# A hybrid decoder trunk: some products of its layers come out transposed, with the weight matrix standing in the array

## The chip, the cores and the metric

One core of a Trainium2 chip runs the whole program. The metric is the device time of one execution in microseconds (us). A change of about 0.3% is the least that runs of this kernel can tell from none.

## The reference, cut to what matters

Two layers (l = 0, 1) over 256 positions of width 1024, in float32. Per layer:

```python
mod = silu(c) @ ada_w[l] + ada_b[l]                 # shift1, scale1, gate1, shift2, scale2, gate2
h = rms_norm(x, norm_mix_w) * (1 + sc1) + sh1
proj = h @ w_in                                     # u,v | fox q,k,v | moba q,k,v | z, xbc | gates
y_a = gmlp(gelu(u), gelu(v))                        # uses u, v by position
y_b = forgetting_attention(q, k, v, f)              # scores q @ k.T: needs q and k with channels on partitions
y_c = moba_attention(rotary(q), rotary(k), v)       # 256 positions are one block: causal attention
y_d = mamba2(z, xbc, dt)                            # convolution along positions: needs channels on partitions
merged = sum(sigmoid(gate_i) * (y_i @ w_branch_i))
x = x + g1 * (merged @ w_out)
h = rms_norm(x, norm_mlp_w) * (1 + sc2) + sh2
x = x + g2 * (relu(h @ mlp_w1) ** 2 @ mlp_w2)       # D_FF = 4096: eight blocks of 512 columns
```

The output is `rms_norm(x)`.

## The kernel before

**Products.** Every large product runs in three float32r matmuls per term: an operand is split into a rounded part `hi` and a rest `lo`, and hi·hi, hi·lo and lo·hi are added in PSUM. The activations are held transposed (128 channels on the partitions, positions along the row) in pairs `xh`, `xl`. The weights stream: a load (`raw`, 512 KB) brings 256 rows by 512 columns of a weight matrix; ScalarE rounds it into `hi` (L363), VectorE subtracts to get `lo` (L365), and TensorE uses the pair. Such a load with its matmuls is called a unit here. `unit_mms` (L415 to L421) does a unit for one half of the positions (t = 0 or 1, 128 positions each): 128 columns of `xh` or `xl` stand in the array as weights, and the 512 columns of `hi` or `lo` move through. A unit has 2 t x 2 j x 3 = 12 matmuls of 512 moving columns, each with its own load of 128 standing columns, and its result has positions on the partitions. `gemm` (L423) chains units into a product (4 units where 1024 rows are summed); `by_tile` takes all units of several products for t = 0 and then for t = 1, so that t = 0 is ready early.

**Where the result is wanted transposed.** Four kinds of results are turned behind the product by `transposes` (L505), four 128 x 128 TensorE transposes into one PSUM bank, twice per product of 512 columns:
- z and the Mamba inputs (`z0` to `z3`, four products per layer): `zx_post` (L667) copies PSUM to SBUF (L671), transposes (`zxT`), and copies out in pieces (L679, L681).
- q and k of the forgetting attention (`fq`, `fk`) and of the other one (`mq`, `mk`): `qk_post` (L593), with transposes named `fqt`, `fkt`, `mqt`, `mkt`.
- each block of the MLP's hidden layer (`w10` to `w17`): `hidden_post` (L900) takes relu and square (L904, L905) to `rl`, transposes to `hd`, and splits into `hh` and `hl` (L502, L503), which stand in the array in the second product (`yps`).

**MLP.** The blocks 0 and 1 of the first product run by tile, while the second half of h is still being normed. From b = 2 on, a turn of the loop does the second product of block b - 2 (four units into `yps`), and then the first product of block b (four units, `w1b`). The blocks 6 and 7 of the second product run by tile at the end.

**Order.** The queue of the loads (SyncE) is in the order of the code; on the other engines a scheduler sets the order at build time. Loads go into a ring of 5 `raw` buffers; `hi` and `lo` have 4 buffers each, and `ahead` (L380) asks for three units in advance. 20 units per layer near its joints borrow other tiles for `hi` and `lo` (`lent`, L287). Beside the weights of the products, 80 loads hold pieces of `ada_w`: VectorE alone uses them, in `ada_step` (L240, L242). They are spread over the stages (24 of them in the MLP of layer 0, 8 in that of layer 1).

Running generators (`start`, `pump`) emit the work behind a product step by step between its successors' units.

Of the kernel before, what the change touches and what calls it, by code (L numbers as in the profile page):

```python
# [7 lines left out]
F32 = mybir.dt.float32  # L8
# [10 lines left out]
NT = 2  # L19
# [119 lines left out]
def trunk_kernel(ctx: ExitStack, tc: tile.TileContext, a: dict, out: bass.AP):  # L139
# [283 lines left out]
    def gemm(key, nk, xs, ps=None, start=True, stop=True, alloc=gps):  # L423
        n = nk // 2
        if ps is None:
            ps = [alloc(f"ps_{key[0]}{key[1]}_{t}") for t in range(NT)]
        for u in range(n):
            i = take(key, 1)[0]
            ahead(i)
            for t in range(NT):  # L430
                unit_mms(i, t, ps[t], xs[t][0], xs[t][1], 2 * u, start and u == 0, stop and u == n - 1)
            pump()
        return ps

    def by_tile(parts):


        got = [take(p[0], p[1]) for p in parts]
        for t in range(NT):
            for (key, n, xs, bank, start_, stop_, after), ids in zip(parts, got):  # L440
                ps = bank(t)
                for u, i in enumerate(ids):
                    ahead(i, got[-1][-1] + 1 if t == 0 else None)
                    unit_mms(i, t, ps, xs[t][0], xs[t][1], 2 * u, start_ and u == 0, stop_ and u == n - 1)
                    pump()
                if after is not None:
                    after(t, ps)
# [43 lines left out]
    def xT_tiles(nm):
        r = []
        for t in range(NT):
            r.append((ap_.tile([P, KT, P], F32R, tag=f"xh{t}", name=f"xh{nm}{t}"),
                      ap_.tile([P, KT, P], F32R, tag=f"xl{t}", name=f"xl{nm}{t}")))
        return r

    def yT_tiles(nm, n, tag):
        return [[mp.tile([P, n, P], F32R, tag=tag, bufs=4, name=f"y{w}{nm}{t}") for w in "hl"] for t in range(NT)]

    def hilo(hi, lo, src):
        s.copy(hi, src)  # L502
# [90 lines left out]
    def qk_post(l, nm, part, ps, tT, rot):  # L593
        tks = []
        for t in range(NT):
            tk = tok(f"{nm}{part}{l}{t}")
            s.activation(tk, ps[t], AF.Copy, scale=0.125 if part == "q" else 1.0)
            if rot:
                k4 = tk.rearrange("p (h c) -> p h c", h=NH)[:, :, 0:16].rearrange("p h (a f) -> p h a f", a=2)
                ra = w2([P, NH, 2, 8], f"ra{part}{l}{t}")  # L600
                rb = w2([P, NH, 2, 8], f"rb{part}{l}{t}")
                cs = rope[:, t, 0, None, :].to_broadcast([P, NH, 16]).rearrange("p h (a f) -> p h a f", a=2)
                sn = rope[:, t, 1, None, :].to_broadcast([P, NH, 16]).rearrange("p h (a f) -> p h a f", a=2)
                v.tensor_tensor(ra, k4, cs, op=ALU.mult)
                v.tensor_tensor(rb, k4[:, :, ::-1, :], sn, op=ALU.mult)
                v.tensor_tensor(k4, ra, rb, op=ALU.add)
            tks.append(tk)
        yield 1
        for t in range(NT):
            tp = transposes(tks[t], f"{nm}{part}t{l}{t}")  # L610
            if t == 0:
                v.tensor_copy(tT[:, :, t * P:(t + 1) * P], tp)
            else:
                s.copy(tT[:, :, t * P:(t + 1) * P], tp)
            yield 0

    def qkv(l, nm, hT, rot):
        tr = []
        for part in ("q", "k"):
            ps = gemm((l, nm + part), KT, hT)  # L620
            tT = mp.tile([P, 4, 2 * P], F32, tag="qk", bufs=2, name=f"{nm}{part}T{l}")
            start(qk_post(l, nm, part, ps, tT, rot), -1)
            tr.append(tT)
        ps = gemm((l, nm + "v"), KT, hT)
        vt = []
        for t in range(NT):
            vt.append(tok(f"{nm}v{l}{t}"))
            s.copy(vt[t], ps[t])
        return tr[0], tr[1], vt
# [37 lines left out]
    def zx_post(l, n, ps, zs, xb):  # L667
        tks = []
        for t in range(NT):
            tk = tok(f"zx{l}{n}{t}")  # L670
            s.copy(tk, ps[t])  # L671
            tks.append(tk)
        yield 1
        for t in range(NT):
            tp = transposes(tks[t], f"zxT{l}{n}{t}")
            for lo_, hi_ in ((0, 2), (2, 4)):
                f0 = 4 * n + lo_
                if f0 < 6:
                    s.copy(zs[:, f0:f0 + 2, t * P:(t + 1) * P], tp[:, lo_:hi_, :])  # L679
                else:  # L680
                    s.copy(xb[:, f0 - 6:f0 - 4, 3 + t * P:3 + (t + 1) * P], tp[:, lo_:hi_, :])  # L681
            yield 0
# [217 lines left out]
    def hidden_post(l, b, pw, hb):  # L900
# [6 lines left out]
        for t in pw:  # L907
            tp = transposes(qs[t], f"hd{l}{b}{t}")
            hilo(hb[t][0], hb[t][1], tp)
            yield 0  # L910

    load_par(0, s)
    fullp = mp.tile([P, KT, 2 * P], F32, tag="s10", bufs=1, name="full0")
    hT = xT_tiles("h0")
    ccol = cst[:, K_C:K_C + KT]
    nr = [norm_sum(0, "a0")]
    cth = sp.tile([P, KT], F32, tag="cth", bufs=1, name="cth")
# [55 lines left out]
    for l in range(L):  # L975
# [64 lines left out]
            zx = [start(zx_post(l, 0, pz, zs, xb), -1)]  # L1040
        start(narrow(l, full, res))
        for n in range(1 if l == 0 else 0, 4):
            ps = gemm((l, f"z{n}"), KT, hT)
            zx.append(start(zx_post(l, n, ps, zs, xb), -1))
        g.memset(xb[:, :, 0:3], 0.0)
        gen_d = mamba(l, zs, xb, yd, res, zx)
        start(gen_d, 4)
# [50 lines left out]
        yc = yT_tiles(f"c{l}", 4, "y3")  # L1098
        gen_c.append(start(attention(f"m{l}", yc, qTm, kTm, vtm, None), 2))
        branch("b", yb, before=lambda: drain(gen_b[0]))  # L1100
        mT = xT_tiles(f"m{l}")

        def merge_T(t, q):
            tp = transposes(mg[t][:, q * 512:q * 512 + 512], f"mT{l}{t}{q}")
# [4 lines left out]
        def merge_gen(t, q):  # L1109
# [3 lines left out]

        branch("c", yc, before=lambda: drain(gen_c[0]),
               last=lambda t, n: start(merge_gen(t, n), 0 if t == 0 else 1))
        h2 = xT_tiles(f"h2{l}")

        def after_o(n):
            def f(t, ps):
# [7 lines left out]


        yps = [[gps(f"yps{l}{t}{n}") for n in range(2)] for t in range(NT)]
        hid = {}  # L1130

        def hidden_tiles(b):
            hid[b] = [[mp.tile([P, 4, P], F32R, tag="y2" if b % 2 else "y3", bufs=4, name=f"h{w}{l}{b}{t}")
                       for w in "hl"] for t in range(NT)]

        gens = []

# [9 lines left out]
        for b in range(2, 9):  # L1147
            for n in range(2) if b < 8 else ():
                p = b - 2
                gemm((l, f"w2{p}{n}"), 4, hid[p], ps=[yps[0][n], yps[1][n]], start=p == 0, stop=False)  # L1150
            if b < 8:
                pw = gemm((l, f"w1{b}"), KT, h2, alloc=xps)
                hidden_tiles(b)
                gen_h = start(hidden_post(l, b, dict(enumerate(pw)), hid[b]), -1)
            if b == 2 and l + 1 < L:
                load_big(l + 1, nc.sync)
            if b == 4 and l + 1 < L:
                start(spatial_sum(l + 1))
        if l + 1 < L:
            nh = xT_tiles(f"h{l + 1}")  # L1160
            nf = mp.tile([P, KT, 2 * P], F32, tag="s10", bufs=1, name=f"full{l + 1}")
            next_h = (nh, nf)

# [102 lines left out]
```

## Time and profile before

| | us |
|---|---|
| median of 3 runs | 1137.05 |
| lowest, highest | 1134.5, 1137.47 |
| the profiled execution's own time | 1135.02 |
| its span in the trace | 1133.3 |
| TensorE matmuls busy, in the span | 1099.9 |
| VectorE busy | 767.7 |
| ScalarE busy | 625.3 |

A matmul is shown from its start to the end of its way through the array, and it overlaps its successor; so what a matmul costs is read from start to start and not from its shown length. A weight load (PEld) begins when the matmul before it begins to stream, and this makes the starts of the loads the sharper clock where matmuls of unlike shapes follow each other.

The stages in the trace, by the names of TensorE's outputs: `u`, `v`, `z` to 101 us, `fq`, `fk`, `fv` to 137, the four branches to 355, `w_out` to 381, the MLP of layer 0 to 582, then the same for layer 1 (MLP from 937 to 1125).

### The profile page before, as it was taken

The numbers are of one execution on the slowest core, as the hardware profiler recorded it, in microseconds if no ns is written. First come the engines' busy times: TensorE is split into PE (matmuls) and PEld (weight loads), VectorE is DVE, ScalarE is ACT, GpSimd is POOL, SyncE is SP. The second block draws the span as 40 slices with busy tenths as digits, with TensorE's granted clock in tenths as the row PEclk, the third lists the DMA queues.
The fourth block names the chain that finished last, engine by engine and source line by source line (L and its number), as shares of the span: only waits on it lengthen the run. The fifth ranks groups of instructions, "written<-read, shape, count | busy, mean of one in ns | idle before, by whom it ended". The sixth has DMA issues, their size and how long they took to land.

```text
span 1133.3 us, 14903 instructions
## 1 busy us (share of the span) xinstructions
PE 1099.9 (97%) x5500; PEld 875.2 (77%) x5500; DVE 767.7 (68%) x1092; ACT 625.3 (55%) x1007; POOL 36.5 (3%) x58
## 2 busy tenths in 40 slices
PE   6999999999999999999899999999999999999997
PEld 4778877877777788887577888787777777888885
DVE  3785857886777856556677567679768586555555
ACT  4556765555654645544464676656555456544453
POOL 0000002000000100000000000110000001000000
PEclk9999999999999999999999999999999999999998
DMA  9865444576666567677745554446666654666661
GB/s 354 339 239 173 167 170 142 193 238 207 213 214 238 191 234 259 227 241 251 268 150 196 183 194 153 165 149 219 217 211 207 225 187 166 206 210 208 200 234 38
DMA packets 65321, 234.52 MB, mean 207 GB/s; under 512 B 7256, under 2 KB 8024, under 8 KB 65248
## 3 DMA queue, kind: packets, MB, share of 16 engines
q1 hardware_dynamic: 64960, 233.30, 60.2%
q8 instruction: 43, 0.70, 0.2%
q10 hardware_dynamic: 288, 0.27, 0.1%
q14 instruction: 30, 0.25, 0.1%
HBM read 232.49 MB, written 1.05 MB: 206 GB/s over the span
## 4 chain that ended last, share of the span: by engine, by line
PE 78%; DMA 10%; DVE 7%; ACT 2%; issue 2%; POOL 1%; DVEq 0%; POOLq 0%; ACTq 0%; SPq 0%
DMA raw<-in_wpk_dram 9%; PE yps L420 4%; PE yps L419 4%; PE yps L421 4%; DVE lo L365 3%; PE ps_1w L420 2%; PE ps_1w L419 2%; PE ps_1w L421 2%; PE ps_1z L419 1%; PE ps_0z L419 1%; PE ps_0w L419 1%; PE ps_0w L420 1%; PE ps_0z L421 1%; PE ps_1z L421 1%; PE ps_0w L421 1%
## 5 line engine op out<-in xcount | busy, mean ns | idle before, releaser
L363 ACT CAST hi<-raw 128x1024 fp32r<-128x1024 f32 x319 | 333.2, 1050 | 321.1 <-PE yps L421 66.4
L365 DVE TENSOR_TENSOR lo<-raw,hi 128x1024 fp32r<-128x1024 f32 x315 | 382.1, 1223 | 168.6 <-ACT hi L363 167.1
L242 DVE SCALAR_TENSOR_TENSOR acc<-raw,csil,acc 128x1024 f32<-128x1024 f32 x70 | 89.8, 1283 | 99.9 <-DMA raw<-in_wpk_dram 99.8
L419 PE MATMUL yps<-hi,hh 128*128 128x512 f32 x232 | 93.9, 405 | 0.3 <-ACT hi L363 0.3
L420 PE MATMUL yps<-lo,hh 128*128 128x512 f32 x232 | 91.6, 396 | 1.5 <-DVE lo L365 1.5
L421 PE MATMUL yps<-hi,hl 128*128 128x512 f32 x232 | 91.6, 395 | 0.0
L420 PEld LDWEIGHTS yps<-lo,hh 128*128 128x128 f32 x232 | 43.6, 188 | 11.8 <-DVE lo L365 2.5
L419 PEld LDWEIGHTS yps<-hi,hh 128*128 128x128 f32 x232 | 43.6, 188 | 11.8 <-issue 1.8
L421 PEld LDWEIGHTS yps<-hi,hl 128*128 128x128 f32 x232 | 43.5, 187 | 10.5
L420 PE MATMUL ps_0w<-lo,xhh 128*128 128x512 f32 x116 | 46.0, 397 | 1.8 <-DVE lo L365 1.8
L419 PE MATMUL ps_0w<-hi,xhh 128*128 128x512 f32 x116 | 46.0, 397 | 0.0
L419 PE MATMUL ps_1w<-hi,xhh 128*128 128x512 f32 x116 | 45.9, 396 | 0.0
L420 PE MATMUL ps_1w<-lo,xhh 128*128 128x512 f32 x116 | 45.9, 396 | 0.0
L421 PE MATMUL ps_0w<-hi,xlh 128*128 128x512 f32 x116 | 45.7, 394 | 0.0
L421 PE MATMUL ps_1w<-hi,xlh 128*128 128x512 f32 x116 | 45.6, 393 | 0.0
L503 DVE TENSOR_TENSOR hl<-hd,hh 128x512 fp32r<-128x512 f32 x32 | 21.9, 684 | 10.1 <-ACT hh L502 10.1
L420 PEld LDWEIGHTS ps_0w<-lo,xhh 128*128 128x128 f32 x116 | 21.9, 188 | 7.8 <-DVE lo L365 3.1
L419 PE MATMUL ps_1z<-hi,xhh 128*128 128x512 f32 x64 | 25.9, 404 | 0.0
L419 PE MATMUL ps_0z<-hi,xhh 128*128 128x512 f32 x64 | 25.7, 402 | 0.0
L419 PEld LDWEIGHTS ps_1w<-hi,xhh 128*128 128x128 f32 x116 | 21.8, 188 | 5.0
L421 PEld LDWEIGHTS ps_1w<-hi,xlh 128*128 128x128 f32 x116 | 21.8, 188 | 5.0
L421 PEld LDWEIGHTS ps_0w<-hi,xlh 128*128 128x128 f32 x116 | 21.8, 188 | 4.9
(591 smaller groups left out, 2566.9 us busy)
## 6 DMA issues: line engine op xcount, KB each, us to landing
raw<-in_wpk_dram SPq DMA_DIRECT2D x436, 512.0 KB, 4.2
x<-in_x_dram SPq DMA_DIRECT2D x2, 512.0 KB
wst<-in_big_dram SPq DMA_DIRECT2D x2, 512.0 KB
out_dram<-xnz SPq DMA_DIRECT2D x4, 256.0 KB
bsb<-in_big_dram SPq DMA_DIRECT2D x2, 256.0 KB
fw<-in_final_norm_w_dram SPq DMA_DIRECT2D x1, 512.0 KB
w<-in_big_dram SPq DMA_DIRECT2D x2, 128.0 KB
cst<-in_cst_dram ACTq DMA_DIRECT2D x1, 185.0 KB
```

The costliest lines, as they stand in the source:

```text
L242: v.scalar_tensor_tensor(acc[l, j], raw, csil[:, k:k + 1], acc[l, j], op0=ALU.mult, op1=ALU.add)
L363: s.copy(hi, raw)
L365: v.tensor_sub(lo, raw, hi.bitcast(F32))
L419: te.matmul(ps, xhi[:, k, :], hi[j], start=first and j == 0, stop=False)
L420: te.matmul(ps, xhi[:, k, :], lo[j], start=False, stop=False)
L421: te.matmul(ps, xlo[:, k, :], hi[j], start=False, stop=last and j == 1)
L503: v.tensor_sub(lo, src, hi.bitcast(F32))
```

## The change

**What comes turned.** `gemm_T` does a unit with the roles exchanged: 128 columns of the weights `hi` or `lo` stand in the array, and all 256 positions of `xh` or `xl` move. A unit has 4 f x 2 j x 3 = 24 matmuls of 256 moving columns, each with its own load of 128 standing columns. The result has channels on the partitions, so that no transpose follows. It replaces `gemm` in 92 units: the blocks `w12` to `w17` of both layers (48), `z1` to `z3` of layer 0 and `z0` to `z3` of layer 1 (28), `fq` and `fk` of both layers (16). With it go 184 of the 128 x 128 transposes: 96 of 128 `hd`, 56 of 64 `zxT`, all 16 `fqt` and all 16 `fkt`.

**What runs behind them.** `turned_post` takes one ScalarE activation per PSUM bank straight to where the result is wanted, `hidden_turned` relu, square and the split per bank. Both begin one pump later than before.

**Tiles.** The four x tiles (`xh`, `xl` of each t) become two tiles over all positions, `xhT` and `xlT`, allocated once; the y and hidden tiles are joined in the same way. A half of the positions is now a slice of them; the places in the tile and the waits that go with them (by region) stay. By the addresses in the built programs, the four old x tiles began 32 bytes past a multiple of 64 bytes, as the `hi` and `lo` of the ring do; `xhT` and `xlT` begin at a multiple of 64, as the y and hidden tiles and the lent `hi` and `lo` do in both kernels.

```diff
+    def gemm_T(key, xs, alloc):
+        ps = [alloc(f"pT_{key[0]}{key[1]}_{q}").rearrange("p (f c) -> p f c", f=2) for q in range(2)]
+        for u in range(KT // 2):
+            i = take(key, 1)[0]
+            ahead(i)
+            hi, lo = ready[i]
+            for f in range(4):
+                o = ps[f // 2][:, f % 2, :]
+                for j in range(2):
+                    k = 2 * u + j
+                    c = slice(f * P, (f + 1) * P)
+                    te.matmul(o, hi[j][:, c], xs[0][:, k, :], start=k == 0 and f % 2 == 0, stop=False)
+                    te.matmul(o, hi[j][:, c], xs[1][:, k, :], start=False, stop=False)
+                    te.matmul(o, lo[j][:, c], xs[0][:, k, :], start=False, stop=k == KT - 1 and f % 2 == 1)
+            pump()
+        return ps
...
+    xall = [cp.tile([P, KT, NT * P], F32R, name=f"x{w}T") for w in "hl"]
+    def by_pos(pair):
+        return [[w[:, :, t * P:(t + 1) * P] for w in pair] for t in range(NT)]
+    def xT_tiles():
+        return by_pos(xall)
...
+    def turned_post(ps, dst, scale=1.0):
+        yield 0
+        for q in range(2):
+            s.activation(dst[q], ps[q], AF.Copy, scale=scale)
+            yield 0
...
+    def hidden_turned(l, b, ps, hb):
+        yield 0
+        for q in range(2):
+            rl = w2([P, 2, NT * P], f"rl{l}{b}{q}")
+            s.activation(rl, ps[q], AF.Relu)
+            s.activation(rl, rl, AF.Square)
+            hilo(hb[0][:, 2 * q:2 * q + 2, :], hb[1][:, 2 * q:2 * q + 2, :], rl)
+            yield 0
...
-            ps = gemm((l, f"z{n}"), KT, hT)
-            zx.append(start(zx_post(l, n, ps, zs, xb), -1))
+            ps = gemm_T((l, f"z{n}"), xall, gps)
+            zx.append(start(turned_post(ps, [zs[:, f:f + 2, :] if f < 6 else xb[:, f - 6:f - 4, 3:3 + NT * P]
+                                             for f in (4 * n, 4 * n + 2)]), -1))
...
-                pw = gemm((l, f"w1{b}"), KT, h2, alloc=xps)
+                pw = gemm_T((l, f"w1{b}"), xall, xps)
                 hidden_tiles(b)
-                gen_h = start(hidden_post(l, b, dict(enumerate(pw)), hid[b]), -1)
+                start(hidden_turned(l, b, pw, whole[b]), -1)
```

On TensorE, in the first unit of block `w12` of layer 0 (`xhh` and `xlh` are the x tiles of t = 0), there stood before:

```order
L419 MATMUL ps_0w_0_3880<-hi_3843,xhh_3339 128x512
L420 MATMUL ps_0w_0_3880<-lo_3844,xhh_3339 128x512
L421 MATMUL ps_0w_0_3880<-hi_3843,xlh_3340 128x512
L419 MATMUL ps_0w_0_3880<-hi_3843,xhh_3339 128x512
L420 MATMUL ps_0w_0_3880<-lo_3844,xhh_3339 128x512
L421 MATMUL ps_0w_0_3880<-hi_3843,xlh_3340 128x512
```

and in the same place now (the standing operand is named last):

```order
L447 MATMUL pT_0w_0_4022<-xhT,hi_3985 128x256
L448 MATMUL pT_0w_0_4022<-xlT,hi_3985 128x256
L449 MATMUL pT_0w_0_4022<-xhT,lo_3986 128x256
L447 MATMUL pT_0w_0_4022<-xhT,hi_3985 128x256
L448 MATMUL pT_0w_0_4022<-xlT,hi_3985 128x256
L449 MATMUL pT_0w_0_4022<-xhT,lo_3986 128x256
```

The two operands have changed places, the moving row is half as long, and the unit has twice as many such rows.

On TensorE, two units later in the second product of layer 0, the transposes of block 2 stood between two units of `yps`:

```order
L419 MATMUL yps_3571<-hi_3941,hh_3705 128x512
L420 MATMUL yps_3571<-lo_3942,hh_3705 128x512
L421 MATMUL yps_3571<-hi_3941,hl_3706 128x512
L508 MATMUL hd_4013<-cst,rl_3961 128x128 x4
L419 MATMUL yps_3570<-hi_3979,hh_3703 128x512
L420 MATMUL yps_3570<-lo_3980,hh_3703 128x512
```

and now the units follow each other:

```order
L419 MATMUL yps_3717<-hi_4119,hh_3847 128x512
L420 MATMUL yps_3717<-lo_4120,hh_3847 128x512
L421 MATMUL yps_3717<-hi_4119,hl_3848 128x512
L419 MATMUL yps_3716<-hi_4161,hh_3847 128x512
L420 MATMUL yps_3716<-lo_4162,hh_3847 128x512
L421 MATMUL yps_3716<-hi_4161,hl_3848 128x512
```

Nothing but the `hd` rows has left this place, and no other row of TensorE is moved past another there.

On VectorE, around block 5 of the MLP of layer 0 (the number behind `raw` counts the loads in the order of their queue; the rows with `acc` use a piece of `ada_w`), before:

```order
L242 SCALAR_TENSOR_TENSOR acc11_4205<-raw203_4529,csil_112,acc11_4205 128x1024
L365 TENSOR_TENSOR lo200_4490<-raw200_4487,hi200_4489 128x1024
L365 TENSOR_TENSOR lo201_4508<-raw201_4505,hi201_4507 128x1024
L242 SCALAR_TENSOR_TENSOR acc10_4137<-raw206_4597,csil_112,acc10_4137 128x1024
L365 TENSOR_TENSOR lo202_4526<-raw202_4523,hi202_4525 128x1024
L365 TENSOR_TENSOR lo204_4557<-raw204_4554,hi204_4556 128x1024
L242 SCALAR_TENSOR_TENSOR acc11_4205<-raw209_4645,csil_112,acc11_4205 128x1024
```

and now:

```order
L242 SCALAR_TENSOR_TENSOR acc11_4428<-raw203_4815,csil_110,acc11_4428 128x1024
L365 TENSOR_TENSOR lo200_4752<-raw200_4749,hi200_4751 128x1024
L365 TENSOR_TENSOR lo201_4782<-raw201_4779,hi201_4781 128x1024
L365 TENSOR_TENSOR lo202_4812<-raw202_4809,hi202_4811 128x1024
L242 SCALAR_TENSOR_TENSOR acc10_4351<-raw206_4890,csil_110,acc10_4351 128x1024
L365 TENSOR_TENSOR lo204_4847<-raw204_4844,hi204_4846 128x1024
L522 TENSOR_TENSOR hl05_4843<-rl050_4862,hh05_4842 128x512
L242 SCALAR_TENSOR_TENSOR acc11_4428<-raw209_4931,csil_110,acc11_4428 128x1024
```

The `lo` of load 202 now stands ahead of the `acc` of load 206 (the same happens to loads 192 and 222), and the rest `hl` of the hidden block needs no transpose and stands earlier.

## Rows read from the trace of the kernel before

**Rows 1.** The page, part 1: engine, busy us (share of the span) x instructions.
```profile
PE 1099.9 (97%) x5500; PEld 875.2 (77%) x5500; DVE 767.7 (68%) x1092; ACT 625.3 (55%) x1007; POOL 36.5 (3%) x58
```

**Rows 2.** The page, part 4: chain that ended last, share by engine.
```profile
PE 78%; DMA 10%; DVE 7%; ACT 2%; issue 2%; POOL 1%; DVEq 0%; POOLq 0%; ACTq 0%; SPq 0%
```

**Rows 3.** Windows: stretch, length, busy by engine (instructions), PE clock, DMA share, GB/s.
```profile
60.00:96.00 36.00, 36.00 (x219) 28.81 (x218) 27.87 (x54) 21.32 (x31) 0.38 (x2) 1.00 0.62 216
503.00:526.00 23.00, 21.84 (x97) 17.08 (x96) 13.80 (x14) 9.75 (x13) 0.00 (x0) 1.00 0.65 228
545.00:562.00 17.00, 13.10 (x52) 7.95 (x52) 12.94 (x13) 11.06 (x16) 0.00 (x0) 0.90 0.84 296
1013.00:1036.00 23.00, 23.00 (x106) 18.75 (x105) 12.95 (x13) 11.60 (x14) 0.00 (x0) 1.00 0.58 206
```

**Rows 4.** Groups by line and shape, TensorE's transposes: xcount | busy us, mean ns | idle.
```profile
L508 PE MATMUL hd<-cst,rl 128*128 128x128 f32 x128 | 19.7, 277 | 1.7 <-ACT rl L905 1.7
L508 PE MATMUL zxT<-cst,zx 128*128 128x128 f32 x64 | 9.6, 272 | 0.0
L508 PE MATMUL fqt<-cst,fq 128*128 128x128 f32 x16 | 2.4, 272 | 0.0
L508 PE MATMUL fkt<-cst,fk 128*128 128x128 f32 x16 | 2.4, 272 | 0.0
```

**Rows 5.** Timeline: start us, length us, instruction; four transposes inside a w1 product.
```profile
403.62 0.60 PE L508 MATMUL hd<-cst,rl 128*128 128x128 f32 x4
...
404.05 0.19 PEld L420 LDWEIGHTS ps_0w<-lo,xhh 128*128 128x128 f32 x1
```

**Rows 6.** Timeline: three matmuls of 256 columns between matmuls of 512, Mamba, layer 0.
```profile
158.20 0.39 PE L837 MATMUL lt<-mask,identb 128*128 128x512 bf16 x1
158.20 0.42 PEld L839 LDWEIGHTS lt<-rr,vb 80*128 80x128 f32 x2
...
158.55 0.19 PEld L845 LDWEIGHTS ea<-rr,onesa 80*128 80x128 f32 x1
158.66 0.28 PE L845 MATMUL ea<-rr,onesa 80*128 80x256 f32 x1
158.66 0.19 PEld L419 LDWEIGHTS ps_0ga<-hi,xhh 128*128 128x128 f32 x1
...
158.78 0.19 PEld L420 LDWEIGHTS ps_0ga<-lo,xhh 128*128 128x128 f32 x1
```

**Rows 7.** Timeline, TensorE: matmuls at both ends of runs of equal ones, four kinds.
```profile
219.40 0.40 PE L419 MATMUL ps_0pd<-hi,yhd 128*128 128x512 f32 x1
...
222.20 0.40 PE L419 MATMUL ps_0pd<-hi,yhd 128*128 128x512 f32 x1
...
402.22 0.40 PE L419 MATMUL ps_0w<-hq,xhh 128*128 128x512 f32 x1
...
403.38 0.39 PE L421 MATMUL ps_0w<-hq,xlh 128*128 128x512 f32 x1
...
979.00 0.39 PE L419 MATMUL ps_1w<-hi,xhh 128*128 128x512 f32 x1
...
981.74 0.39 PE L419 MATMUL ps_1w<-hi,xhh 128*128 128x512 f32 x1
...
1108.00 0.39 PE L419 MATMUL yps<-hq,hh 128*128 128x512 f32 x1
...
1109.13 0.40 PE L421 MATMUL yps<-hq,hl 128*128 128x512 f32 x1
```

**Rows 8.** Timeline, VectorE, MLP of layer 0: in brackets, idle time and its end.
```profile
502.04 1.28 DVE L242 SCALAR_TENSOR_TENSOR acc<-raw,csil,acc 128x1024 f32<-128x1024 f32 x1 [3.70 <-DMA raw<-in_wpk_dram]
503.24 2.35 DVE L365 TENSOR_TENSOR lo<-raw,hi 128x1024 fp32r<-128x1024 f32 x2
509.30 1.28 DVE L242 SCALAR_TENSOR_TENSOR acc<-raw,csil,acc 128x1024 f32<-128x1024 f32 x1 [3.70 <-DMA raw<-in_wpk_dram]
```

More of the change, by code (lines that the diff above doesn't have):

```diff
@@ L489, in norm_T @@
             hilo(hi[:, 4 * q:4 * q + 4, :], lo[:, 4 * q:4 * q + 4, :], f)
[L491 to L496, printed above, removed]
+    xall = [cp.tile([P, KT, NT * P], F32R, name=f"x{w}T") for w in "hl"]
[3 more added lines that the diff above has]
+        return by_pos(xall)
     def yT_tiles(nm, n, tag):
-        return [[mp.tile([P, n, P], F32R, tag=tag, bufs=4, name=f"y{w}{nm}{t}") for w in "hl"] for t in range(NT)]
+        return by_pos([mp.tile([P, n, NT * P], F32R, tag=tag, bufs=2, name=f"y{w}{nm}") for w in "hl"])
     def hilo(hi, lo, src):
@@ L619, in qkv @@
         for part in ("q", "k"):
-            ps = gemm((l, nm + part), KT, hT)
-            tT = mp.tile([P, 4, 2 * P], F32, tag="qk", bufs=2, name=f"{nm}{part}T{l}")
-            start(qk_post(l, nm, part, ps, tT, rot), -1)
+            if rot:
+                ps = gemm((l, nm + part), KT, hT)
+                tT = mp.tile([P, 4, 2 * P], F32, tag="qk", bufs=2, name=f"{nm}{part}T{l}")
+                start(qk_post(l, nm, part, ps, tT, rot), -1)
+            else:
+                ps = gemm_T((l, nm + part), xall, gps)
+                tT = mp.tile([P, 4, 2 * P], F32, tag="qk", bufs=2, name=f"{nm}{part}T{l}")
+                start(turned_post(ps, [tT[:, 2 * q:2 * q + 2, :] for q in range(2)], 0.125 if part == "q" else 1.0), -1)
             tr.append(tT)
@@ L910, in hidden_post @@
             yield 0
+    def hidden_turned(l, b, ps, hb):
[6 more added lines that the diff above has]
+            yield 0
     load_par(0, s)
     fullp = mp.tile([P, KT, 2 * P], F32, tag="s10", bufs=1, name="full0")
-    hT = xT_tiles("h0")
+    hT = xT_tiles()
     ccol = cst[:, K_C:K_C + KT]
@@ L1100, in trunk_kernel @@
         branch("b", yb, before=lambda: drain(gen_b[0]))
-        mT = xT_tiles(f"m{l}")
+        mT = xT_tiles()
         def merge_T(t, q):
@@ L1115, in trunk_kernel @@
                last=lambda t, n: start(merge_gen(t, n), 0 if t == 0 else 1))
-        h2 = xT_tiles(f"h2{l}")
+        h2 = xT_tiles()
         def after_o(n):
@@ L1129, in trunk_kernel @@
         yps = [[gps(f"yps{l}{t}{n}") for n in range(2)] for t in range(NT)]
-        hid = {}
+        hid, whole = {}, {}
         def hidden_tiles(b):
-            hid[b] = [[mp.tile([P, 4, P], F32R, tag="y2" if b % 2 else "y3", bufs=4, name=f"h{w}{l}{b}{t}")
-                       for w in "hl"] for t in range(NT)]
+            whole[b] = [mp.tile([P, 4, NT * P], F32R, tag="y2" if b % 2 else "y3", bufs=2, name=f"h{w}{l}{b}")
+                        for w in "hl"]
+            hid[b] = by_pos(whole[b])
         gens = []
@@ L1159, in trunk_kernel @@
         if l + 1 < L:
-            nh = xT_tiles(f"h{l + 1}")
+            nh = xT_tiles()
             nf = mp.tile([P, KT, 2 * P], F32, tag="s10", bufs=1, name=f"full{l + 1}")
```

## The prediction

> **What bounds the kernel now.** I read the page first. TensorE is busy for 1099.9 us of 1133.3 [rows 1], and the chain of work that ended last lies on it for 78% [rows 2]; VectorE (767.7) and ScalarE (625.3) have room. Since a busy TensorE is not a TensorE at its peak, I then read windows: in the z products (60 to 96) and in the MLP of layer 1 (1013 to 1036) it is busy for the whole stretch at full clock [rows 3], so that a matmul taken away there is taken off the end. One stage is different. Late in the MLP of layer 0 it idles: 1.2 us of 503 to 526 and 3.9 us of 545 to 562, where the clock also fell (0.90 on average) [rows 3]. VectorE stands still there for 3.70 us at a time before an `acc` [rows 8]: it has gone to a later load while two earlier ones, already landed, hold their buffers. So in that stage the loads set the pace, and not TensorE.
>
> **What goes: 184 transposes.** All lie in TensorE's queue inside its products. Their shown length (272 to 277 ns [rows 4]) is that of their way through the array and not their cost. The cost is in the timeline: the first of four starts at 403.62, and the product goes on streaming at 404.05, when the load for its second matmul begins [rows 5]. That is 0.43 us for four. 184 transposes are 46 groups: 46 x 0.43 = 19.8 us off TensorE. Few wait for anything today (1.7 us idle before all 128 `hd`, none before the others [rows 4]), so nothing else goes with them.
>
> **What comes: shorter matmuls, twice as many.** The moving columns of a unit stay the same (12 x 512 = 24 x 256). What counts is what a matmul costs beyond its columns, and whether a weight load of 128 columns fits behind one of 256 columns.
> - Today's unit with x standing: 979.00 to 981.74 is 2.74 us for 12, 0.228 each [rows 7]. In some w1 blocks the trace has the slower spacing of the y units, 2.80. I take 2.76 over the 92 units.
> - The turned unit: the trace has three float32r matmuls of 256 columns in a row. A load begins when the matmul before it begins to stream (158.66 in both rows), and loads begin at 158.55, 158.66 and 158.78: 0.115 us each [rows 6]. With the first of the three it is 158.20 to 158.78 less 0.23 for the bf16 matmul of 512: 0.35, or 0.117 each. The loads are shown 0.19 long and still begin 0.11 to 0.12 apart, so they overlap each other; and the last of them has all 128 rows. No row has 24 of them in succession. I take 0.118, the upper side of these: 24 x 0.118 = 2.83, 0.07 more than now, and 92 x 0.07 = +6.4 us.
> - Bounds: half of today's best spacing (0.114) gives 2.74 and -1.8 us; if every matmul pays on top the 0.005 by which the two kinds of today's units differ, and a little more (0.124), it is 2.98 and +19.9 us. The rows lie near the lower end.
>
> The Trainium skill (page TensorE: Matmul & The Clock Gate, section LDWEIGHTS (loading the stationary operand)) gives a load as its columns over 1.2 GHz, an estimated 107 ns for 128 columns, as long as 256 columns take to stream at 2.4 GHz. By that alone a unit would be 24 x 107 ns = 2.57 us and the turned units would gain 17 us; the rows at 115 to 120 ns are not that low, and I go by them.
>
> **What moves: the place of x.** Every product that keeps x standing reads it from a new place. The trace has pairs that differ in this: units whose moving operand begins 32 bytes past a multiple of 64 and whose standing one does too take 2.74 (979.00), those with standing y tiles at a multiple of 64 take 2.80 (219.40 to 222.20, 12 matmuls), x with lent weights, the mixed case turned about, 0.232 each (402.22 to 403.38, five), and both at a multiple of 64 0.226 (1108.00 to 1109.13, five) [rows 7]. I read this as: unlike places cost about 0.005 per matmul. The change makes 128 units unlike (gates 64, `mq`, `mk`, `mv` 24, `fv` 8, `u`, `v` and the first `z0` 16, half of `w_out` and of `w10`, `w11` 16) and 20 lent units alike. 12 x 0.005 = 0.06 per unit, of which I take 0.045 since some run at 2.80 today: 128 x 0.045 = 5.8, less 20 x 12 x 0.006 = 1.4: **+4.4 us**, between 0 (the reason is another property of the tiles) and +6.3. The turned units are unlike too; so are the `ea` matmul of [rows 6] and its neighbours, so that the price of 0.118 holds it.
>
> **What has one answer.** ScalarE and VectorE lose the copies of z, fq and fk and keep the relu, square and split of the hidden blocks at equal sizes; they are not the bound, so nothing is counted. The later start of the posts by one pump costs nothing where the result is used one product later or more: hidden block b is used after four units of `yps` and four of the next block, over 20 us. The shortest cover is block 7, wanted four half units (5.5 us) behind its product: six ScalarE steps and one of VectorE, which I estimate at 0.6 us each, 4.2 us, fit; without that cover up to 2 us per layer would be lost. The waits for parts of x go by region and stay.
>
> **The MLP of layer 0.** Blocks 4 to 7 of that stage lie where loads set the pace. TensorE's gain there, 8 groups x 0.43 less 16 x 0.07 = 2.3 us, would become waiting. Against it, in three places `lo` now goes ahead of an `acc` (loads 192, 202, 222). A buffer is then free one VectorE step earlier behind each of these `acc`, and the step is about 1.15 us (2.35 for two [rows 8]): up to 3.4 us off the path of the loads. I set the two against each other at zero; range -1.5 to +2.3.
>
> **The sum.** -19.8 + 6.4 + 4.4 = **-9.0 us**. The profiled execution took 1135.0 itself (span 1133.3), so 1126.0 for it; it lies 2 us under the median of 1137.05 and inside the runs' spread, so I carry the difference to the median: 1128.0.
>
> **Rivals.**
> - *The spacing of a turned matmul is 0.124* (slower). Place: the 92 units; nothing in the trace shows a long run of short matmuls with a load each, and there a load and a matmul are nearly of one length, so neither hides the other's delays. Price +19.9 instead of +6.4: +4.5, 1141.5. It decides at 0.122, where the 15.4 us that are left of the transposes are used up. Against it: the spacings of [rows 6], 0.115 and 0.117, are below it.
> - *It stops at 0.121 to 0.122*, and the trade is even: 2.92 x 92 against 2.76 x 92 is +14.7, net -0.7, 1136. For it: only 0.003 more than I take.
> - *The loads eat the gain in the MLP of layer 0*: 2.3 us less, -6.7, 1130.4. For it: TensorE idles there now; against it the three better places in the order.
> - *Weight loads do not hide at all.* Each turned matmul would then pay its load, which four transposes show at 0.43 / 4 = 0.108: 24 x 0.226 = 5.42, +2.66 x 92 = +245 us, 1373. The rows speak against it: three matmuls with three loads take 0.35. The Trainium skill (same page, part 3, section The mechanism) says that a load overlaps a matmul under way only when its row group differs, and all loads here use all rows; by that rule today's matmul of 512 columns would not start every 0.228, with its load beginning as the one before streams, so the trace disagrees.
>
> That the transposes might stay is excluded by the order of the built program, which has only the 32 of `w10`, `w11`, the 8 of the first `z0` and those of other stages.
>
> **How the numbers follow.** Chances: the forecast 0.54, the loads 0.10 (both faster by over 0.3%, which is 3.4 us and about what can be told from no change), the even trade 0.20, the spacing of 0.124 or more 0.14, loads in the open 0.02. So faster 0.64, same 0.20, slower 0.16. The predicted time is the forecast's, 1128. The range: the low end is 0.115 per matmul (no cost) with the order's gain and half of the cost of the place of x, -19.8 + 0 + 2.2 - 0.5 = -18, 1119; the high end is the slower rival's 1141. Outside are open loads and anything worse than 0.124.
>
> **What would show it.** In the profile of the changed kernel: TensorE with 920 matmuls more (5500 + 92 x 12 - 184); loads of the turned units beginning 0.115 to 0.12 apart, and a unit in 2.76 to 2.88; `gd` or `gb` units at 2.80 in place of 2.74; the z stage and fq, fk together shorter by about 7 x (0.86 - 0.28) + 4 x (0.86 - 0.28) = 6.4 us; each of blocks 2 to 7 in layer 1 shorter by 0.6 us. Wrong it would be by turned units over 2.92, by new idle time in front of them (a wait for `hi`, `lo` or a PSUM bank), or by a layer-0 MLP that is as long as before.

## The result, and the profile after

The changed kernel takes 1119.87 us (median; 1115.5 to 1120.94). Its ratio to the kernel before is 0.9857, with a 95% interval from 0.9834 to 0.988: 16.2 us less, between 13.6 and 18.9. Forecast were 9.0 less. So the direction was right and the size was not.

The page after, part 1 (as [rows 1]) and part 4, the chain that ended last by engine (as [rows 2]):

```profile
PE 1089.8 (98%) x6420; PEld 913.2 (82%) x6420; DVE 767.5 (69%) x1088; ACT 619.7 (55%) x975; POOL 37.2 (3%) x58
...
PE 81%; DMA 8%; DVE 7%; ACT 2%; issue 2%; POOL 1%; DVEq 0%; POOLq 0%; ACTq 0%; SPq 0%
```

TensorE has 920 matmuls more, as predicted, and is 10.1 us less busy while the span is 15.8 shorter: about a third of the gain is idle time that has gone. That the chain has 8% of DMA in place of 10% points the same way.

The timeline of TensorE after, the first turned unit of a block of layer 1 and its successor's first matmul (as [rows 6]), and below it a product with x standing (`ga` of layer 1, as [rows 7]):

```profile
984.86 0.28 PE L447 MATMUL pT_1w<-xhT,hi 128*128 128x256 f32 x1
984.98 0.28 PE L448 MATMUL pT_1w<-xlT,hi 128*128 128x256 f32 x1
985.10 0.28 PE L449 MATMUL pT_1w<-xhT,lo 128*128 128x256 f32 x1
...
987.70 0.28 PE L447 MATMUL pT_1w<-xhT,hi 128*128 128x256 f32 x1
```
```profile
684.63 0.40 PE L419 MATMUL ps_1ga<-hi,xhT 128*128 128x512 f32 x1
...
686.50 0.40 PE L421 MATMUL ps_1ga<-hi,xlT 128*128 128x512 f32 x1
```

24 turned matmuls take 987.70 - 984.86 = 2.84 us, 0.118 each. Eight with x standing take 686.50 - 684.63 = 1.87, 0.234 each, where the unit of [rows 7] had 0.228.

I took the start of every matmul in both traces, grouped them by what stands in the array, and counted what a spacing has above 1.13 times the usual one as waiting (10.4 us less, of which 3.4 are the steps behind the transposes). This gives where the time between the first and the last matmul went (15.5 us less):

| part | predicted, us | from the two traces, us |
|---|---|---|
| 184 transposes | -19.8 | -16.4 in their own spacing (20.0 to 3.6), -3.4 in the longer step of the matmul behind each group (46 x (0.43 - 4 x 0.089)) |
| 92 turned units, 2208 matmuls at 118.3 ns for 1104 at 230.1 | +6.4 | +7.2 |
| x at its new place: 1596 matmuls from 230.1 to 233.1 ns, 180 lent ones from 233.5 to 229.6 | +4.4 | +4.1 |
| waiting | 0 | -7.0 |

(Five of the 20 lent units use tiles that the trace also calls `hi` and `lo`; their 60 matmuls are among the 1596.)

The three terms of TensorE came out within 1 us. The miss is waiting. By stage (from the first matmul of a stage to the first of the next) it lies in two places. The MLP of layer 0 went from 201.0 to 194.5 us, of which TensorE's own terms explain 3.2 (12 groups at 0.43, less 24 units at 0.08). Branch c of layer 1 (`pc`, up to `w_out`) went from 16.7 to 13.5 with no instruction of it changed. Windows of these two stages, of the kernel before and after (columns as in [rows 3]):

```profile
380.90:581.80 200.90, 194.36 (x881) 154.06 (x880) 129.00 (x143) 103.23 (x143) 4.64 (x7) 0.99 0.69 236
895.10:911.80 16.70, 13.07 (x61) 9.84 (x60) 11.76 (x14) 8.80 (x11) 0.00 (x0) 1.00 0.65 231
```
```profile
380.10:574.70 194.60, 189.83 (x1122) 164.49 (x1121) 128.60 (x143) 104.28 (x143) 5.61 (x7) 0.99 0.73 244
886.30:899.80 13.50, 12.78 (x61) 9.91 (x60) 12.03 (x14) 8.84 (x11) 0.00 (x0) 1.00 0.73 224
```

VectorE does the same work in both (129 us), and the loads move the same bytes in less time: 244 GB/s for 194.6 us in place of 236 for 200.9.

### The profile page after: what moved, and what is told of

The parts are those of the page before. It is cut to its first block, busy times and chain, and to the rows that moved or that the text cites. A ratio compares the mean times of both kernels' runs of the same rounds, so it can differ in the third digit from the quotient of the medians.

```text
span 1117.5 us, 16674 instructions
## 1 busy us (share of the span) xinstructions
PE 1089.8 (98%) x6420; PEld 913.2 (82%) x6420; DVE 767.5 (69%) x1088; ACT 619.7 (55%) x975; POOL 37.2 (3%) x58
## 4 chain that ended last, share of the span: by engine, by line
PE 81%; DMA 8%; DVE 7%; ACT 2%; issue 2%; POOL 1%; DVEq 0%; POOLq 0%; ACTq 0%; SPq 0%
DMA raw<-in_wpk_dram 7%; PE yps L419 4%; PE yps L420 4%; PE yps L421 4%; DVE lo L365 2%; PE pT_1w L447 2%; PE pT_1w L448 2%; PE pT_1w L449 2%; PE pT_1z L447 1%; PE pT_1z L448 1%; PE pT_1z L449 1%; PE pT_0w L449 1%; PE pT_0w L447 1%; PE pT_0w L448 1%; PE pT_0z L447 1%
## 5 line engine op out<-in xcount | busy, mean ns | idle before, releaser
L449 PE MATMUL pT_0w<-xhT,lo 128*128 128x256 f32 x192 | 54.2, 282 | 0.1
L447 PE MATMUL pT_1w<-xhT,hi 128*128 128x256 f32 x192 | 54.0, 281 | 0.0
L447 PE MATMUL pT_0w<-xhT,hi 128*128 128x256 f32 x192 | 54.0, 281 | 0.0
L449 PE MATMUL pT_1w<-xhT,lo 128*128 128x256 f32 x192 | 53.9, 281 | 0.0
L448 PE MATMUL pT_1w<-xlT,hi 128*128 128x256 f32 x192 | 53.9, 281 | 0.0
L448 PE MATMUL pT_0w<-xlT,hi 128*128 128x256 f32 x192 | 53.9, 281 | 0.0
L449 PEld LDWEIGHTS pT_0w<-xhT,lo 128*128 128x128 f32 x192 | 36.2, 188 | 0.5 <-DVE lo L365 0.5
L448 PEld LDWEIGHTS pT_1w<-xlT,hi 128*128 128x128 f32 x192 | 36.2, 188 | 0.3
L448 PEld LDWEIGHTS pT_0w<-xlT,hi 128*128 128x128 f32 x192 | 36.2, 188 | 0.3
L447 PE MATMUL pT_1z<-xhT,hi 128*128 128x256 f32 x128 | 36.3, 284 | 0.0
```

What stands on the lines that cost most here:

```text
L447: te.matmul(o, hi[j][:, c], xs[0][:, k, :], start=k == 0 and f % 2 == 0, stop=False)
L448: te.matmul(o, hi[j][:, c], xs[1][:, k, :], start=False, stop=False)
L449: te.matmul(o, lo[j][:, c], xs[0][:, k, :], start=False, stop=k == KT - 1 and f % 2 == 1)
```

## Experiments: what the order of acc and lo is worth

The theory after the result: the three places where VectorE does `lo` of a load ahead of the `acc` of a later one are what shortened the waits in the MLP of layer 0. I had priced them at up to 3.4 us. The rival: turned blocks free buffers earlier, or the one profile was lucky.

**The order alone, in the kernel before** (`los[i]` holds the `lo` of load i; the `acc` is only put behind it in VectorE's queue):

```diff
-            ada_step(*key, raw)
+            with tc.issue_after(los[{196: 192, 206: 202, 226: 222}[i]]) if i in (196, 206, 226) else nullcontext(): ada_step(*key, raw)
```

> The kernel before with only the order on VectorE changed in the MLP of layer 0: the lo of loads 192, 202 and 222 ahead of the acc of 196, 206 and 226, as the changed kernel has it. Theory A (that order is what shortened the waits for loads in this stage): the stage of the layer-0 MLP shortens by about 3.5 us and the kernel with it, -3 to -4 us. Theory B (the waits went because the turned blocks free hi, lo and raw earlier, or by chance in the one profile): 0 within 1.5 us.

Measured: 0.9934 [0.9911, 0.9958], 7.5 us less by the ratio (4.8 to 10.1; 6.5 by the medians). So the order does it, and it is worth about twice what was expected. The MLP of layer 0 takes 194.2 us (201.0 before), all other stages are within 0.6 of before. The timeline around the first place, of the kernel before (with ScalarE's `hi` of load 192) and of this one (in brackets: idle time, and what ended it):

```profile
474.27 1.05 ACT L363 CAST hi<-raw 128x1024 fp32r<-128x1024 f32 x1 [1.70 <-PE ps_0w L421]
473.75 2.35 DVE L365 TENSOR_TENSOR lo<-raw,hi 128x1024 fp32r<-128x1024 f32 x2
480.25 1.29 DVE L242 SCALAR_TENSOR_TENSOR acc<-raw,csil,acc 128x1024 f32<-128x1024 f32 x1 [4.15 <-DMA raw<-in_wpk_dram]
481.46 2.35 DVE L365 TENSOR_TENSOR lo<-raw,hi 128x1024 fp32r<-128x1024 f32 x2
```
```profile
472.61 3.49 DVE L365 TENSOR_TENSOR lo<-raw,hi 128x1024 fp32r<-128x1024 f32 x3
478.88 1.28 DVE L242 SCALAR_TENSOR_TENSOR acc<-raw,csil,acc 128x1024 f32<-128x1024 f32 x1 [2.78 <-DMA raw<-in_wpk_dram]
480.08 1.22 DVE L365 TENSOR_TENSOR lo<-raw,hi 128x1024 fp32r<-128x1024 f32 x1
```

Before, `hi` of load 192 was done at 475.3, and its `lo` stood behind an `acc` that waited 4.15 us for its own load: it ran at 481.5. In the other order it is the third of the `lo` from 472.61, and done at 476.1. Its buffer is free 6.6 us earlier by the clock of each trace (482.7 and 476.1), 5.4 when the lead that this trace already had at the `lo` of load 191 (1.2 us) is taken off; load 198, counted in the queue, was issued at 476.1 in place of 481.6. Nothing had to be computed faster.

What TensorE waited for `lo` and `hi` in this stage, by its waits there (total us, times, longest), in the kernel before:

```profile
PE ps_0w L420 <- DVE lo L365: 1.8, 3, 1.0
PE yps L420 <- DVE lo L365: 1.5, 2, 0.9
PE yps L419 <- ACT hi L363: 0.3, 1, 0.3
```

That is 3.6 us, and none of it is left in this run. The changed kernel has one such wait left (`yps`, 0.5 us).

**The reverse, in the changed kernel:** the `acc` of 196, 206 and 226 back ahead of those `lo`.

```diff
+        if i in (192, 202, 222):
+            while st["d"] <= i + 4: load_one()
+            ada_step(*units[i + 4][1], ready[i + 4])
+            with tc.issue_after(st["a"]): v.tensor_sub(lo, raw, hi.bitcast(F32))
```

> The changed kernel with the order on VectorE at the three places of the layer-0 MLP put back as before: the acc of loads 196, 206 and 226 ahead of the lo of 192, 202 and 222. If that order is worth in the changed kernel what it is worth in the old one (7.5 us there): about 1127, 0.993 to 0.995 of the kernel before, since the changed kernel had given some of it back in a new wait at sst (3.7 us) that would shrink again. If the turned blocks shorten the waits for loads by themselves: within 1.5 us of the changed kernel, 0.986.

Measured: 0.9899 [0.9865, 0.9933], 1124.67 us, 4.8 more than the changed kernel, between the two answers expected. The order seems worth less here than the 7.5 us in the kernel before, but the two values lie within each other's noise, and why they differ is not shown (the long wait at the end of the stage, `sst` below, stands in both traces). The MLP of layer 0 takes 198.0 us, and TensorE waits for `lo` there again, 2.8 us:

```profile
PE pT_0w L453 <- DVE lo L367: 1.3, 1, 1.3
PE yps L424 <- DVE lo L367: 0.9, 1, 0.9
PE pT_0w L453 <- DVE lo L369: 0.6, 1, 0.6
```

What is left against the kernel before is 9.4 us by the medians (11.5 by the ratio): the forecast of 9.0, for which the order counted as nothing, lies inside its interval. It also speaks against the rival that the loads eat TensorE's gain in this stage: 201.0 to 198.0, one profile each, is close to TensorE's own 3.2.

**Without most loads of ada_w, both kernels.** Of the 80 later loads of `ada_w`, 60 and their VectorE steps are left out (k = 1 to 6 of each piece).

```diff
-        kind, key, _ = units[i]
+        kind, key, _ = units[i]; skip = kind == "ada" and 0 < key[2] < KT - 1
+        if skip: return
...
-            ada_step(*key, raw)
+            if raw is not None: ada_step(*key, raw)
```

> The kernel before without 60 of the 80 later loads of ada_w and their VectorE steps (k = 1 to 6 of each piece; the modulation is wrong by that). If loads and the acc ahead of lo set the pace in the layer-0 MLP and at branch c: the waits there go, -8 to -12 us (13.1 us of waiting in the layer-0 MLP, of which some 5 stay at the norm's transposes, hd and sst; 3 us at branch c of layer 1). If those waits have another cause: -2 us or less.

> The changed kernel without the same 60 loads and steps (the modulation is wrong by that). If what the change brought beyond TensorE's own sum (-19.8 + 7.2 + 4.1 = -8.5 us) was waiting for loads, then without that waiting the two kernels differ by the sum alone: 7 to 9.5 us between this and the kernel before without these loads. If the rest came from something else, they differ by 15 to 17 us as the full kernels do.

Measured: 1118.67 us (0.9849 [0.9819, 0.9879]) and 1110.2 us (0.977 [0.974, 0.98]). The loads and their steps cost the kernel before 15 us by the medians, more than the 8 to 12 expected, and the changed one 10. The two differ by 8.5 us, which is TensorE's own sum (-19.8 + 7.2 + 4.1): without these loads their waiting hardly differs. So the rest of the 16.2 hangs on these loads.

**Branch c of layer 1.** Here no order had changed. Before, VectorE at this stage's two `acc`, and TensorE waiting for a `lo` behind the second:

```profile
889.99 1.28 DVE L242 SCALAR_TENSOR_TENSOR acc<-raw,csil,acc 128x1024 f32<-128x1024 f32 x1 [4.40 <-DMA raw<-in_wpk_dram]
891.19 3.49 DVE L365 TENSOR_TENSOR lo<-raw,hi 128x1024 fp32r<-128x1024 f32 x3
...
898.86 1.29 DVE L242 SCALAR_TENSOR_TENSOR acc<-raw,csil,acc 128x1024 f32<-128x1024 f32 x1 [3.85 <-DMA raw<-in_wpk_dram]
900.06 1.22 DVE L365 TENSOR_TENSOR lo<-raw,hi 128x1024 fp32r<-128x1024 f32 x1
...
901.34 0.50 PE L420 MATMUL ps_1pc<-lo,yhc 128*128 128x512 f32 x1 [1.62 <-DVE lo L365]
```

After, the same two waits of VectorE are 2.41 and 1.40 us:

```profile
878.41 1.28 DVE L242 SCALAR_TENSOR_TENSOR acc<-raw,csil,acc 128x1024 f32<-128x1024 f32 x1 [2.41 <-DMA raw<-in_wpk_dram]
...
886.51 1.28 DVE L242 SCALAR_TENSOR_TENSOR acc<-raw,csil,acc 128x1024 f32<-128x1024 f32 x1 [1.40 <-DMA raw<-in_wpk_dram]
```

The edit puts three `acc` behind older `lo` in the kernel before:

```diff
+BEHIND = {352: 348, 356: 353, 359: 354}
-            ada_step(*key, raw)
+            with tc.issue_after(los[BEHIND[i]]) if i in BEHIND else nullcontext(): ada_step(*key, raw)
```

> The kernel before with only three steps moved on VectorE, at branch c of layer 1: the acc of loads 352, 356 and 359 behind the lo of 348, 353 and 354. That stage (from the first matmul of pc to the first of w_out) took 16.7 us before and 13.5 in the changed kernel, though nothing of it was changed, and between 13.5 and 16.6 in the variants that have the old order there; with acc behind lo at these places and 22 others it took 12. If the order of acc and lo paces the stage: 12 to 13 us there, and the whole 3 to 5 us less than before, 0.996 to 0.997. If the stage waits for the landing of the loads themselves: 15 to 17 us as before, and the whole within 1.5 us.

Measured: 0.9968 [0.9953, 0.9984], 3.6 us less, the stage 12.1 us with TensorE busy throughout:

```profile
895.50:907.60 12.10, 12.10 (x57) 9.78 (x56) 10.24 (x13) 7.46 (x9) 0.00 (x0) 1.00 0.65 218
```

So this order makes the stage sensitive to when a load lands. Why it took 13.5 us in the changed kernel is not settled. The six other runs of the changed kernel with the same order here took 14.0 to 16.6 (15.2 on average) with one profile each, and the kernel before and the run with the order alone 16.7 and 16.1. So the 13.5 is the luckiest of seven: of the 16.2 us, between 1 and 3 can be this.

## Experiments: the place of the operands

**x 32 bytes further:**

```diff
+    cp.tile([P, 8], F32, name="pad0")
     xall = [cp.tile([P, KT, NT * P], F32R, name=f"x{w}T") for w in "hl"]
+    cp.tile([P, 8], F32, name="pad1")
```

> The changed kernel with both x tiles moved by 32 bytes, to 32 past a multiple of 64, where the old x tiles and the hi and lo of the ring begin; nothing else changes. Theory (unlike places of the two operands cost about 3 ns per matmul of 512): the 1596 matmuls with x standing go from 233.1 ns back to about 230.1 (-4.8 us) and the 180 on lent weights from 229.6 to 233.5 (+0.7): -4.1 us against the changed kernel, so about -20 us against the kernel before; the turned matmuls (x moving, weights standing) become alike too and may fall from 118.3 to 115 to 117, which would be 3 to 7 us more. Rival (the slower spacing comes from the joined tiles, their row length of 256 or their reads, not from the place): the x-standing matmuls stay at 233 ns and the time at about -16 us.

Measured: 0.9827 [0.9803, 0.9851], 3.9 us less than the changed kernel by the medians; the intervals of the two ratios overlap. The spacings show it: x standing 233.1 to 230.1 ns, lent 229.6 to 233.4, turned 118.3 to 117.0, and y and hidden as they were (233.3, 233.2). So the place was the reason, as the prediction read it. The three changes make 6.8 us in the trace; the medians show less, and 1.8 of it went at branch c of layer 1 (15.3 us there in place of 13.5).

**The ring moved to x's place** (`hi`, `lo`, x, y and hidden all at a multiple of 64):

```diff
     xall = [cp.tile([P, KT, NT * P], F32R, name=f"x{w}T") for w in "hl"]
+    cp.tile([P, 8], F32, name="pad0"); ap_.tile([P, 8], F32, tag="pad1", bufs=1, name="pad1")
```

> The changed kernel with the ring of raw, hi and lo moved by 32 bytes to a multiple of 64 (and the tiles behind it left where they are), so that both operands of every unit begin at a multiple of 64. Theory of the place: matmuls with x standing 233.1 to about 229.5 ns (1596 of them, -5.7 us), with y standing (432) and hidden standing (695) also to about 229.5 (-1.7 and -2.6): -10 us against the changed kernel, about -26 us against the kernel before, and more if the turned matmuls gain as well. Rival: no spacing changes, about -16 us.

Measured: 0.9759 [0.9734, 0.9785], 1107.59 us, 12.3 less than the changed kernel. Spacings: x standing 229.7, y 228.5, hidden 227.2, turned 115.7 ns. The second product of layer 1, TensorE's timeline of the changed kernel and of this one:

```profile
976.22 0.40 PE L421 MATMUL yps<-hi,hl 128*128 128x512 f32 x1
...
984.62 0.40 PE L421 MATMUL yps<-hi,hl 128*128 128x512 f32 x1
```
```profile
968.95 0.39 PE L419 MATMUL yps<-hi,hh 128*128 128x512 f32 x1
...
973.48 0.39 PE L421 MATMUL yps<-hi,hl 128*128 128x512 f32 x1
```

From the first to the last start shown, 36 matmuls take 8.40 us (0.233 each) in the first, 20 take 4.53 (0.2265 each) in the second.

## Experiments: the parts, and a wait that didn't matter

**Only z, fq and fk turned; only w12 to w17 turned.** Each puts the other part's `gemm` and post back.

```diff
-                pw = gemm_T((l, f"w1{b}"), xall, xps)
+                pw = gemm((l, f"w1{b}"), KT, h2, alloc=xps)
...
-                start(hidden_turned(l, b, pw, whole[b]), -1)
+                start(hidden_post(l, b, dict(enumerate(pw)), hid[b]), -1)
```

> The changed kernel with the blocks w12 to w17 back as before (x standing, transposes hd), so that only z, fq and fk come turned; tiles as in the changed kernel. TensorE alone: 88 transposes less (22 groups of 0.43 us, -9.5), 44 turned units at 0.08 us more (+3.5), 2172 matmuls with x standing at 3.0 ns more (+6.5), lent units -0.7: -0.2 us. If the waits for loads became shorter with the turned w1 blocks, the time is that, within 1.5 us of the kernel before, up to -3 us if the waits at the joint of layer 1 (branch c) go with z, fq and fk; if they became shorter everywhere for another reason, -7 us.

> The changed kernel with z, fq and fk back as before (x standing, transposes), so that only the blocks w12 to w17 come turned; it has the changed kernel's order on VectorE in the layer-0 MLP. TensorE alone: 96 transposes less (24 groups of 0.43, -10.3), 48 turned units at 0.08 more (+3.8), 2124 matmuls with x standing at 3.0 ns more (+6.4), lent units -0.7: -0.8 us. If the order is worth here what taking it away cost in the changed kernel (4.8 us): -5 to -6, ratio 0.995. If the turned blocks bring nothing beyond TensorE: -0.8, ratio 0.999. Together with the part that turns only z, fq and fk (0.998) and the move of the places counted once, the parts should give the whole.

Measured: 0.9978 [0.9963, 0.9994] (-2.5 us) and 0.9938 [0.9918, 0.9958] (-7.0 us). The first keeps the old order in the MLP of layer 0 (200.6 us there), the second has the new one (191.1). Their sum, -9.5, holds the price of x's place twice; with 7.4 us of it taken off it is -16.9, close to the whole, though each part is known to 2 us only.

**The wait at `sst`.** The changed kernel has a new long wait at the end of the MLP of layer 0. TensorE and ScalarE there:

```profile
551.54 1.03 ACT L363 CAST hi<-raw 128x1024 fp32r<-128x1024 f32 x1
552.47 0.63 ACT L947 ACTIVATE rl<-rl 128x512 f32<-128x512 f32 x1
553.01 1.03 ACT L363 CAST hi<-raw 128x1024 fp32r<-128x1024 f32 x1
553.94 0.61 ACT L521 CAST hh<-rl 128x512 fp32r<-128x512 f32 x1
554.46 0.58 ACT L270 COPY ssr<-ssp 128x512 f32<-128x512 f32 x1
555.09 1.11 PE L274 MATMUL sst<-cst,ssr 128*128 128x128 f32 x4 [3.27 <-ACT ssr L270]
555.85 0.77 PE L419 MATMUL yps<-hq,hh 128*128 128x512 f32 x1
556.43 0.63 PE L420 MATMUL yps<-hq,hh 128*128 128x512 f32 x1
556.85 0.63 PE L421 MATMUL yps<-hq,hl 128*128 128x512 f32 x1
...
558.49 0.39 PE L419 MATMUL yps<-hq,hh 128*128 128x512 f32 x1
...
559.86 0.40 PE L419 MATMUL yps<-hi,hh 128*128 128x512 f32 x1
```

TensorE stands 3.27 us, and runs at the lower of its two clocks behind it (1.2 GHz: 0.42 us from start to start). The window from 554 to 560 has a granted clock of 0.72:

```profile
554.00:560.00 6.00, 4.91 (x17) 4.13 (x18) 2.17 (x4) 1.04 (x3) 0.00 (x0) 0.72 0.67 236
```

Six matmuls take 2.64 us there (555.85 to 558.49) and the next six 1.37 (558.49 to 559.86). The edit asks for `sst` four pumps later:

```diff
-        yield 1
+        yield 5 if (l, j) == (1, 1) else 1
```

> The changed kernel with the transposes sst of the last ada piece of layer 0 handed out four pumps later, which puts them behind five half units of yps in TensorE's queue in place of before them; ScalarE's copy ssr stays where it is. Theory: the 3.7 us for which TensorE stands there, waiting for ssr behind two hi and the square of block 7 in ScalarE's queue, go, and with them the lower clock behind it (six matmuls at 0.43 us in place of 0.23, 1.2 us): -4 to -5 us against the changed kernel, about 0.982 of the kernel before. Rival: the wait moves to the next unit (its hq or the hidden block 7 late, or nta behind a later ab): 0 to -1 us, 0.986.

Measured: 0.987 [0.9837, 0.9903]: no gain, the rival. (The execution in its profile took 1125.14 us, the longest of its six; only the places of the waits are read from it.) In TensorE's timeline the wait at `sst` is gone, and shorter ones stand behind it that the changed kernel didn't have:

```profile
556.63 0.50 PE L419 MATMUL yps<-hq,hh 128*128 128x512 f32 x1 [1.41 <-ACT hh L521]
...
557.98 0.54 PE L421 MATMUL yps<-hq,hl 128*128 128x512 f32 x1 [0.61 <-DVE hl L522]
...
582.19 0.66 PE L495 MATMUL nta<-cst,xna 128*128 128x128 f32 x4 [0.70 <-DVE xna L490]
```

The `hh` of hidden block 7 stands behind the same `hi` in ScalarE's queue, and its `hl` behind that; both are wanted there. `ssr` was only the first to be waited for.

## Experiments: both findings together

The changed kernel, and the kernel before, each with everything at a multiple of 64 and with 25 `acc` behind a `lo` that had run 2 us or more after it was ready:

```diff
+BEHIND = {90: 86, 98: 94, 141: 136, 166: 162, 183: 180, 186: 182, 189: 187, 193: 191, 196: 194, 199: 197, 203: 201, 206: 204, 209: 207, 213: 211, 216: 214, 219: 217, 223: 221, 226: 224, 315: 311, 318: 314, 338: 334, 349: 346, 352: 348, 356: 353, 359: 354}
```

> The changed kernel with both operands at a multiple of 64 (as the run with the moved ring) and, at 25 places of both layers, the acc of a piece of ada_w behind one or two lo that had been ready more than 2 us before it ran. Theory (an acc that waits for its load at the head of VectorE's queue holds up lo, and with it TensorE and the ring): the layer-0 MLP loses most of the 5 to 6 us of load waiting that are left, branch c of layer 1 some 2: 4 to 7 us less than the run with the moved ring (0.976), so 0.970 to 0.973. Rival (acc runs later, holds its buffer longer, and the loads after it come later): 0.976 or worse.

> The kernel before with the same two things: ring and x at a multiple of 64, and acc behind lo at the same 25 places. Places: 432 y and 695 hidden matmuls at 5 ns less, 180 lent ones at 4 ns less, 2700 with x standing at 230.1 to about 229.7: -8 us; order: -8 to -11 us; together 0.983 to 0.986. With both out of the way, what is left between this and the changed kernel with the same two things is TensorE's own: -19.8 for the transposes, and 2208 x 115.7 ns less 1104 x 229.7 ns = +1.9 for the shorter matmuls: -18 us. If the transposes are worth less than 0.43 us a group once nothing else waits, the two are closer.

Measured: 1096.27 us, 0.9667 [0.9638, 0.9696], and 1116.99 us, 0.9842 [0.9814, 0.9871]. The first beats both kernels: 23.6 us less than the changed one, and a little more than expected. From the page of the changed kernel and of this one, part 5, the group of the `acc` (busy, mean ns | idle before, and its end):

```profile
L242 DVE SCALAR_TENSOR_TENSOR acc<-raw,csil,acc 128x1024 f32<-128x1024 f32 x70 | 89.9, 1284 | 93.2 <-DMA raw<-in_wpk_dram 93.1
```
```profile
L242 DVE SCALAR_TENSOR_TENSOR acc<-raw,csil,acc 128x1024 f32<-128x1024 f32 x70 | 89.7, 1282 | 45.3 <-DMA raw<-in_wpk_dram 45.1
```

The idle time of VectorE ahead of an `acc` is halved, the MLP of layer 0 takes 186.7 us (190.4 in the other), and branch c of layer 1 takes 12.0 (11.9). The two kernels differ by 20.7 us; expected were 18, from -19.8 for the transposes and +1.9 for the shorter matmuls. That fits a group of four transposes at 0.43 us where waiting is largely gone; what the 2.7 us beyond it are is not shown.

## Why the prediction was right and wrong, point by point

- **Transposes, -19.8: right.** The two traces (-16.4 and -3.4) and the pair without loads agree, and the pair with both findings fits. The shown length of 277 ns, which would have given 50 us, was rightly left aside.
- **Turned matmuls at 0.118: right** (118.3 ns over 2208). Three matmuls in a row [rows 6] were enough to foresee it, and both rivals at 0.121 and more fell, as did loads in the open. The Trainium skill (page TensorE: Matmul & The Clock Gate, section LDWEIGHTS (loading the stationary operand)) gives a load as its columns over 1.2 GHz, an estimated 107 ns for 128 columns. The four transposes, each with such a load, take 0.108 apiece [rows 5], which agrees; the turned matmuls did not get as low, with 115.7 at best.
- **The place of x, +4.4: right** in size (+4.1) and in reason, which the run with x moved by 32 bytes shows.
- **The MLP of layer 0, "I set the two against each other at zero": wrong**, and this is the step that failed. Its two sides were 2.3 us of TensorE's gain lost and "up to 3.4 us" won by the order. The loss didn't come. The order is worth 7.5 us in the kernel before and 4.8 in the changed one, and the prediction had put both sides together at nothing. I had priced each place at VectorE's step, 1.15 us, for "a buffer is then free one VectorE step earlier". But the `acc` that stood ahead of `lo` didn't cost its step: it cost its step and the idle time ahead of it, which stood in the row that I had quoted, 3.70 [rows 8]. The three waited 4.15, 3.70 and 2.65 us; with their steps, I estimate from these that the buffers come free up to 14.0 us earlier in all. TensorE gains only the part of that for which it would have waited, so 3.4 was no upper bound, and 7.5 lies inside 14.0.
- **Waits elsewhere, nothing counted: wrong by 1 to 3 us** at branch c of layer 1. I looked for load-paced stages in one place only; the same pattern, an `acc` waiting 4.40 us with ready `lo` behind it, stood here as well.
- **The cover of block 7, "fit": wrong.** In layer 0 two `hi` and `ssr` share ScalarE's queue with its six steps, and its `hh` and `hl` come after TensorE is there. It costs little against the kernel before, which waited near the same place for `hd` (1.66 us).
- **Two sums of the rivals and the range don't come out.** Loads in the open put +245 in the place of +6.4 and not on top of it, which gives 1367 and not 1373. The low end of the range takes 0.5 us for the order where 1.5 had been named as its bound, so it would be 1118. Neither touches the forecast.

Together: -8.5 of TensorE's own, -4.8 of the order and -1 to -3 at branch c make -14.3 to -16.3, where -16.2 was measured (13.6 to 18.9 less). The last of the three has only single profiles behind it, so that up to 2 us stay open.

## What to carry to other kernels

On VectorE, whose instructions ran in the order of their queue, an `acc` that waited for its transfer held up the ready `lo` behind it for its whole wait (4.15 us at the first place). When a change swaps two such instructions, even as a side effect of a scheduler, price the swap at the idle time shown ahead of the waiting one plus its length, and look along the whole trace for more of the same. And look at the addresses of both operands of a product: two pads of 32 bytes, with no work saved, gave 11 to 12 us here.

## What the hardware showed that I had not expected

- Turned matmuls depend on the place too: 118.3 ns with x and weights 32 bytes apart (modulo 64), 117.0 with both at 32, 115.7 with both at 0.
- With 512 columns: 233.1 to 233.5 for unlike places, 230.1 for both at 32, 227.2 to 229.7 for both at 0. Why x standing stays at 229.7 and hidden standing reaches 227.2 at like places is open.
- After 3.27 us of standing still, TensorE ran six matmuls in 2.64 us that take 1.37 at the higher clock, so that this wait cost over a third more than its own length.
